# Decoder layer with a product-key expert FFN on one core: the second expert product over lists of experts in use, with rows fetched by index

## The chip, the core and the metric

The kernel runs on one core of a Trainium2 chip. The metric is the device time of one execution in microseconds (us). A run of the program is also profiled; the span in the profile goes from the first to the last instruction and is a little shorter than the time of the execution that it belongs to.

## What is computed

The reference is one decoder layer on 256 tokens of width 1024 (two attention-like mixers, a projection, a LayerNorm, then the expert FFN). The change is in the expert FFN. Each token has 8 heads; each head picks 16 of 16,384 experts by product keys, so there are 256 x 128 = 32,768 (token, expert, gate) choices:

```
s = einsum('thpk,pnk->thpn', q, sub_keys)              # two halves p, 128 keys n
top_s, top_i = top_k(s, 16)
cand_s = top_s[:, :, 0, :, None] + top_s[:, :, 1, None, :]     # 16 x 16 candidates
cand_i = top_i[:, :, 0, :, None] * 128 + top_i[:, :, 1, None, :]
best_s, best_pos = top_k(cand_s, 16)
experts = take_along_axis(cand_i, best_pos);  gates = softmax(best_s)
hid = gelu(einsum('chkd,cd->chk', u_tab[experts], x))
y   = einsum('chk,chkd->cd', gates * hid, v_tab[experts])
```

Then e = (p @ W_ple) * sigmoid(h @ W_pg + b_pg), and the output is LayerNorm(alpha * h + f + e), with f the y above.

## The kernel before

All weights are streamed. A unit of streaming is an *item* of 512 KB: `do_load` (L92) brings it from DRAM into a tile `raw` (4 buffers), `do_hi` (L103) makes its high part `hi` on ScalarE (ACT; line L110) and `do_lo` (L113) the low part `lo = raw - hi` on VectorE (DVE; line L123). A product of two float32 operands is three TensorE (PE) matmuls, hi*hi, hi*lo and lo*hi (`mm3`, L180), into PSUM. The program is a list of *steps*, one per item. The emission loop at the end writes, for each step, the loads, high parts (3 steps ahead) and low parts (2 steps ahead) by `advance`, then the step's matmuls, then what follows the step before. There is no scheduler: the order of the text is the order on each engine.

Work beside the stream comes in two ways. `stages` holds generators that go on by one `yield` per step. `queue` holds generators that yield an estimate of their DVE time; `run_queue(AUX_BUDGET)` lets each step take so much of it.

The steps in order: v, u, values, q/k, four projections, the output projection (`w_out`, 8 steps; its `wo_before` first finishes all `stages`), the per-layer gate (`w_pg`, 8 steps), the expert queries (`w_q`, 16 steps), the first expert product (128 steps) and the second (128 steps).

First expert product, `uexp_mm`: step i computes u_(i,j) . h_t for the 128 experts (i, j), all 256 tokens, with 24 matmuls of 256 columns; GELU (L802) puts two steps' result into the table H in SBUF. During `w_q` and the first half of these steps `topk_task` (two tasks, one for each 128 tokens) finds the experts and gates.

Gates, `g_task`: for 16 tokens at a time DVE builds one-hot matrices (A over j, B over i, times the gate in two float16 parts Bh and Bl: L815 to L822), PE multiplies them (L828, L829) to a dense gate matrix, and DVE multiplies that into H (L833). There are 32 such tasks, half of them beside the last 64 steps of the first product, half beside the first 64 steps of the second.

Second expert product: step i takes V rows of experts (i, 0..127) as one plain 512 KB load, `wsplit` makes high and low parts of H for two steps (L144 on ACT, L145 on DVE; tiles `wsp_*`), and `vexp_mm` (L885) does 12 matmuls of 512 columns: 2 token tiles x 2 column halves x 3. All 128 steps run, whether an expert is in use or not. The last 3 items are multiplied token tile by token tile, and LayerNorm 2 follows.

All loads and stores are issued by SyncE (SP, "SPq" in the profile); GpSimd (POOL) issues none.

## Time and profile before

| | |
|---|---|
| median of 3 runs | 1099.8 us (1099.3 to 1100.41) |
| span of the profiled execution | 1097.7 us |
| PE busy | 1085.3 us (99%), granted clock 0.997 of full |
| DVE busy | 819.3 us (75%) |
| ACT busy | 522.3 us (48%) |
| POOL busy | 4.4 us |
| moved by DMA | 205.3 MB, 187 GB/s |

The profile shows one execution. The profiled execution's own time is not given apart from its span; the median of the runs is 2.1 us above the span. Busy time counts instructions and not bytes; matmuls are pipelined, so the duration of one (282 ns) is longer than the distance between two starts.

### The profile page before, as it was taken

The page shows a single profiled execution, that of the slowest core. Times are in us where ns is not written, and L with a number is a line of the kernel's source. Part 1 is how long each engine was busy: PE and PEld are TensorE (multiplying, and loading weights), DVE is VectorE, ACT ScalarE, POOL GpSimd, SP SyncE. Part 2 cuts the span into 40 slices and gives each one's busy share as a digit, 9 for nine tenths or more (in the row PEclk, how much of TensorE's full clock was granted, in tenths as well). Part 3 has the DMA queues.
Part 4 walks back from the last instruction along what each step waited for, and adds up shares of the span by engine and source line. Part 5 has one row for each costly group of instructions (what it writes and reads, how often), then busy time and mean ns, then how long its engine had stood idle before and what let it go on. Part 6 is the DMA issues. An engine that isn't in the chain of part 4 may idle for free.

```text
span 1097.7 us, 19871 instructions
## 1 busy us (share of the span) xinstructions
PE 1085.3 (99%) x7985; PEld 989.4 (90%) x7985; DVE 819.3 (75%) x1429; ACT 522.3 (48%) x689; POOL 4.4 (0%) x7
## 2 busy tenths in 40 slices
PE   8999999999999999999999999999999999999996
PEld 6989999988999999999999999988888888888885
DVE  6875656577788989994878787689898975555556
ACT  6535655545445544454444434444444444444442
POOL 0000000000000000000000000000000000000000
PEclk9999999999999999999999999999999999999998
DMA  7856456774645556555555555554555555755551
GB/s 274 306 175 239 146 167 195 255 244 151 213 158 172 189 175 195 190 189 179 171 174 173 173 161 174 173 182 159 178 169 173 173 175 190 268 189 185 186 189 58
DMA packets 58576, 205.30 MB, mean 187 GB/s; under 512 B 6603, under 2 KB 8948, under 8 KB 58100
## 3 DMA queue, kind: packets, MB, share of 16 engines
q1 hardware_dynamic: 58484, 204.04, 56.5%
q8 instruction: 62, 1.02, 0.4%
q14 instruction: 30, 0.25, 0.1%
HBM read 201.91 MB, written 3.68 MB: 187 GB/s over the span
## 4 chain that ended last, share of the span: by engine, by line
PE 98%; DVE 1%; DMA 1%; SPq 0%; ACT 0%; issue 0%; DVEq 0%
PE acc L182 60%; PE y L885 32%; PE misc L828 1%; PE misc L829 1%; PE misc L694 1%; DMA raw<-in_w_v 1%; PE misc L388 0%; PE misc L488 0%; PE misc L466 0%; SPq L99 0%; DVE end L963 0%; PE misc L483 0%; DVE est L954 0%; DVE end L953 0%; PE misc L465 0%; PE misc L489 0%
## 5 line engine op out<-in xcount | busy, mean ns | idle before, releaser
L110 ACT CAST hi<-raw 128x1024 fp32r<-128x1024 f32 (+1 forms) x362 | 378.7, 1047 | 455.3 <-PE acc L182 219.5
L123 DVE TENSOR_TENSOR lo<-raw,hi 128x1024 fp32r<-128x1024 f32 (+1 forms) x362 | 440.2, 1218 | 151.6 <-PE acc L182 55.0
L182 PE MATMUL acc<-h_hi,hi 128*128 128x256 f32 x1152 | 324.9, 282 | 0.0
L182 PE MATMUL acc<-h_lo,hi 128*128 128x256 f32 x1152 | 322.2, 280 | 0.0
L182 PE MATMUL acc<-h_hi,lo 128*128 128x256 f32 x1152 | 321.9, 279 | 0.0
L182 PEld LDWEIGHTS acc<-h_hi,hi 128*128 128x128 f32 x1152 | 216.5, 188 | 0.0
L182 PEld LDWEIGHTS acc<-h_lo,hi 128*128 128x128 f32 x1152 | 216.4, 188 | 0.0
L182 PEld LDWEIGHTS acc<-h_hi,lo 128*128 128x128 f32 x1152 | 216.1, 188 | 0.0
L885 PE MATMUL y<-hi,wsp_hl 128*128 128x512 f32 x512 | 168.9, 398 | 0.0
L885 PE MATMUL y<-hi,wsp_hh 128*128 128x512 f32 x496 | 163.4, 398 | 0.0
L885 PEld LDWEIGHTS y<-hi,wsp_hl 128*128 128x128 f32 x512 | 96.4, 188 | 23.3
L885 PEld LDWEIGHTS y<-hi,wsp_hh 128*128 128x128 f32 x496 | 93.4, 188 | 22.5
L885 PE MATMUL y<-lo,wsp_hl 128*128 128x512 f32 x256 | 100.7, 393 | 0.0
L885 PE MATMUL y<-lo,wsp_hh 128*128 128x512 f32 x248 | 97.5, 393 | 0.0
L182 PE MATMUL acc<-xh,hi 128*128 128x256 f32 x320 | 92.2, 288 | 0.0
L182 PE MATMUL acc<-xh,lo 128*128 128x256 f32 x320 | 90.6, 283 | 0.0
L182 PE MATMUL acc<-xl,hi 128*128 128x256 f32 x320 | 90.6, 283 | 0.0
L182 PEld LDWEIGHTS acc<-xl,hi 128*128 128x128 f32 x320 | 61.5, 192 | 0.2
L182 PEld LDWEIGHTS acc<-xh,hi 128*128 128x128 f32 x320 | 61.4, 192 | 0.2
L182 PEld LDWEIGHTS acc<-xh,lo 128*128 128x128 f32 x320 | 61.4, 192 | 0.0
L815 DVE TENSOR_TENSOR A<-iota,dup_j 128x1024 f16<-128x1024 f16 x64 | 43.9, 686 | 20.1 <-PE misc L829 20.1
L885 PEld LDWEIGHTS y<-lo,wsp_hl 128*128 128x128 f32 x256 | 48.3, 189 | 10.6
(210 smaller groups left out, 1257.3 us busy)
## 6 DMA issues: line engine op xcount, KB each, us to landing
raw<-in_peer_uT SPq DMA_DIRECT2D x128, 512.0 KB, 3.8
raw<-in_peer_v SPq DMA_DIRECT2D x128, 512.0 KB, 4.2
raw<-in_w_qk SPq DMA_DIRECT2D x16, 512.0 KB, 4.3
raw<-in_w_q SPq DMA_DIRECT2D x16, 512.0 KB, 4.0
raw<-in_w_u SPq DMA_DIRECT2D x8, 512.0 KB, 6.1
raw<-in_w_vv SPq DMA_DIRECT2D x8, 512.0 KB, 4.6
raw<-in_w_pa SPq DMA_DIRECT2D x8, 512.0 KB, 3.7
raw<-in_w_ga SPq DMA_DIRECT2D x8, 512.0 KB, 4.2
```

What stands on the lines that cost most here:

```text
L110: nc.scalar.copy(parts[i][0][:, c], raws[i][:, c])
L123: nc.vector.tensor_sub(lo[:, c], r[:, c], hi[:, c].bitcast(F32))
L182: nc.tensor.matmul(ps, l, r, start=start and i == 0, stop=stop and i == 2)
L694: nc.tensor.matmul(sp[:, t, :], q[:, t * 128:(t + 1) * 128], keysT[:, j % 2, :], start=True, stop=True)
L815: nc.vector.tensor_tensor(v4(A), io(0, 128), bcs("j", 128), op=OP.is_equal)
L828: nc.tensor.matmul(ps[:, t, :], A[:, t, :], Bh[:, t, :], start=True, stop=False)
L829: nc.tensor.matmul(ps[:, t, :], A[:, t, :], Bl[:, t, :], start=False, stop=True)
L885: nc.tensor.matmul(cell["Y"][t][c], w[:, wp, j, t * 128:(t + 1) * 128], v[q][:, c, :], start=i == 0 and wp == 0 and q == 0, stop=i == NK - ...
```

## The change

1. A table HG in DRAM holds, for each expert and token tile of 128 tokens, 128 values of gelu(u.h) and 128 gates. `fill_task`, a stage from step 16 on, writes zeros to the gate half: 43 times two DMAs of up to 128 x 3 pieces of 512 bytes (192 KB), one pair every second step; what is left when `wo_before` finishes all stages is issued there.
2. GELU results go to HG by two DMAs per two steps (`uexp_post`, L970) instead of a tile in SBUF.
3. `topk_task` hands out results after 4 and after 8 heads. `scatter_gates` issues, on POOL, one indirect DMA with addition per (head, k): 128 gates of 4 bytes to 128 addresses. That is 4 batches of 64; the first DMA of a head waits until all 16 of the head before have landed.
4. `mask_task` makes one-hot matrices of the chosen experts on DVE (64 of 128x1024) and multiplies them on PE (256 matmuls of 128 columns): how often each token tile uses each expert. `list_task` turns that into three lists (used by tile 0 alone, by tile 1 alone, by both), numbers the members by triangular matmuls, and `slot_rows` (128 matmuls and 256 small DVE instructions) writes for each list position the expert's row number. Both go through `queue`, whose budget is now 1.45.
5. `w_pg` is split: 4 steps stay, 4 come after the first expert product.
6. The second expert product has 102 steps (*slots*): 50 for experts used by both tiles, 26 for each list of one tile, in the order both, tile 0, both, tile 1. A slot's 128 rows of V come by an indirect DMA on POOL (`do_load`, L114), its rows of HG by another (`hg_load`, L1010, 6 slots ahead). `wprep` multiplies gate and value on DVE (L1019) and splits the product (L164 on ACT, L165 on DVE). A slot of both has 12 matmuls, a slot of one tile 6.
7. From the first `w_pg` step on there are 11 raw buffers instead of 4 (`ring`). V rows are not asked for before the lists exist (`load_cap`).
8. If the list of both is longer than 50 slots, a branch (`overflow`, `tc.If`) works off up to 78 more slots one by one. Its condition is a count read into a register of every engine.
9. The dense gate matrix (`g_task`) and the tiles H are gone. The residual `res` stays in SBUF instead of going to DRAM and back.

The diff, cut to its core (lines with "..." stand for what is left out):

```diff
+NX = NK * NK
+ROWS = NX + 128
+ROW = 2 * T
+CAP_A, CAP_B = 26, 50
+SLOTS = 2 * CAP_A + CAP_B
+COLG = 8
+LISTG = 4
+FILL = 3
+HG_AHEAD = 6
+RING = 7
...
-AUX_BUDGET = 1.35
+FILL_AT = 16
+AUX_BUDGET = 1.45
...
-            r = stream.tile(items[i][1], F32, name="raw", tag="raw", bufs=RAW_BUFS)
-        for c in cuts(i):
-            nc.sync.dma_start(r[:, c], items[i][0][:, c])
+            pool, tag, bufs = ring[ring_pos[0] % len(ring)]
+            ring_pos[0] += 1
+            r = pool.tile(items[i][1], F32, name=tag, tag=tag, bufs=bufs)
+        if i in row_lists:
+            nc.gpsimd.indirect_dma_start(r.rearrange("p a b -> p (a b)"), None, items[i][0],
+                                         bass.IndirectOffsetOnAxis(ap=row_lists[i](), axis=0))
+        else:
+            for c in cuts(i):
+                nc.sync.dma_start(r[:, c], items[i][0][:, c])
...
-            while done["load"] <= last and sum(i not in x_items for i in range(done["lo"], done["load"])) < RAW_BUFS:
+            end = last if load_cap[0] is None else load_cap[0]
+            while done["load"] <= end and sum(i not in x_items for i in range(done["lo"], done["load"])) < len(ring):
...
+    HG = dram.tile([ROWS, 2, 2, 128], F32, name="HG")
+    def fill_task():
+        for r in (slice(0, 1), slice(NX + 1, ROWS)):
+            n = r.stop - r.start
+            nc.sync.dma_start(HG[r, :, 0, :], zero[:n, None, :].to_broadcast([n, 2, 128]))
+        rows = HG[:, :, :, :].rearrange("(p r) t w c -> p r t w c", p=128)
+        for r in range(0, ROWS // 128, FILL):
+            n = min(FILL, ROWS // 128 - r)
+            for t in range(2):
+                nc.sync.dma_start(rows[:, r:r + n, t, 1, :], zero[:, None, :].to_broadcast([128, n, 128]))
+            yield
+            yield
...
+        nc.sync.dma_start(kc, a["kc"])
+        nc.sync.dma_start(kcol, a["kcol"])
...
-        cell["H"] = {}
-        h0, cell["h0_es"] = open_pool("h0")
-        cell["h0"] = h0
-        cell["H"][0] = h0.tile([128, HALF, T], F32, name="H0", tag="H0")
+        more, cell["more_es"] = open_pool("more")
+        cell["more"] = more
+        ring.extend([(more, "raw2", RING)] * RING)
+        ring_pos[0] = len(ring) - RING
...
+    def scatter_gates(t, hf, gidx, gates):
+        for h in range(4 * hf, 4 * hf + 4):
+            before, scattered[t] = scattered[t], []
+            for k in range(TOPK):
+                c = TOPK * h + k
+                ins = nc.gpsimd.indirect_dma_start(
+                    gview[TOPK * t + k].rearrange("r t w (c o) -> (r t w c) o", o=1),
+                    bass.IndirectOffsetOnAxis(ap=gidx[:, c:c + 1], axis=0),
+                    gates[:, c:c + 1], None, compute_op=OP.add).ins
+                if k == 0:
+                    for p in before:
+                        tc.add_manual_dep(ins, p, SYNC, reason="another head may add to the same gate")
+                scattered[t].append(ins.name)
...
+            nc.vector.scalar_tensor_tensor(ex, ij[:, 0, :], float(NK), ij[:, 1, :], op0=OP.mult, op1=OP.add)
+            nc.vector.tensor_scalar(gidx[:, cc], ex, float(ROW), kcol[:, t:t + 1], op0=OP.mult, op1=OP.add)
+            scatter_gates(t, hf, gidx, gates.rearrange("p a b -> p (a b)"))
+            yield 0.2
...
+    def mask_task():
+        counts = bank((128, 2, 128))
+        cell["counts"] = counts
+        v4 = lambda x: x.rearrange("p t (i two) -> p t i two", two=2)
+        io = iota.rearrange("p (i two) -> p i two", two=2)[:, None].to_broadcast([128, COLG, 64, 2])
+        todo = None
+        for g in range(2 * 128 // COLG + 1):
+            new = None
+            if g < 2 * 128 // COLG:
+                t, c0 = divmod(g * COLG, 128)
+                new = [t, c0]
+                for p, n in ((1, "A"), (0, "B")):
+                    oh = tk.tile([128, COLG, 128], F16, name=n, tag=n, bufs=2)
+                    nc.vector.tensor_tensor(v4(oh), io, pairs[t][:, p, c0:c0 + COLG, None, :].to_broadcast(
+                        [128, COLG, 64, 2]), op=OP.is_equal)
+                    new.append(oh)
+                    yield 0.7
+            if todo:
+                t, c0, A, B = todo
+                for c in range(COLG):
+                    nc.tensor.matmul(counts[:, t, :], A[:, c, :], B[:, c, :], start=c0 + c == 0,
+                                     stop=c0 + c == 127)
...
+    def slot_rows(kdiv, kmod, n, rows, pair):
+        ps = bank()
+        todo = None
+        for i0 in range(0, NK + LISTG, LISTG):
+            new = None
+            if i0 < NK:
+                P, S = pair(i0)
+                for k in range(LISTG):
+                    i = i0 + k
+                    nc.vector.tensor_scalar(P[:, k, :], iof, kmod[:, i:i + 1], None, op0=OP.is_equal)
+                    nc.vector.tensor_scalar(S[:, k, :n], iof[:, :n], kdiv[:, i:i + 1], evals[:, i:i + 1],
+                                            op0=OP.is_equal, op1=OP.mult)
+                yield 1.0
+                new = (i0, P, S)
+            if todo:
+                j0, P, S = todo
+                for k in range(LISTG):
+                    nc.tensor.matmul(ps[:, :n], P[:, k, :], S[:, k, :n], start=j0 + k == 0, stop=j0 + k == NK - 1)
+            todo = new
+        nc.vector.tensor_copy(rows, ps[:, :n])
+
...
+        cell["vrow"] = cell["more"].tile([128, SLOTS], U32, name="vrow")
+        cell["grow"] = cell["more"].tile([128, SLOTS], U32, name="grow")
+        nc.vector.tensor_scalar(cell["vrow"], rows, -1.0, 0.0, op0=OP.add, op1=OP.max)
+        for t in range(2):
+            c = slice(CAP_A * t, CAP_A * (t + 1))
+            nc.vector.tensor_scalar(cell["grow"][:, c], rows[:, c], 2.0, float(t), op0=OP.mult, op1=OP.add)
+        nc.vector.tensor_copy(cell["grow"][:, 2 * CAP_A:], rows[:, 2 * CAP_A:])
+        load_cap[0] = None
...
-    def g_task(pair, hf):
...
-                nc.tensor.matmul(ps[:, t, :], A[:, t, :], Bh[:, t, :], start=True, stop=False)
-                nc.tensor.matmul(ps[:, t, :], A[:, t, :], Bl[:, t, :], start=False, stop=True)
...
-            hv = cell["H"][hf][:, :, t0:t0 + TOKG]
-            nc.vector.scalar_tensor_tensor(hv, ps.rearrange("p t i -> p i t"), 1.0 / GSC, hv,
-                                           op0=OP.mult, op1=OP.mult)
...
+        h = cell["more"].tile([128, 2, T], F32, name="hid", tag="hid", bufs=3)
+        nc.scalar.activation(h, ps, AF.Gelu)
+        for k in range(2):
+            r = (i - 1 + k) * NK + 1
+            nc.sync.dma_start(hview[r:r + NK, :, 0, :], h[:, k, :].rearrange("p (t c) -> p t c", t=2))
...
+    def v_open():
+        drain_queue()
+        cell["tk_es"].close()
+        vp, cell["vp_es"] = open_pool("vp")
+        cell["vp"] = vp
+        cell["end"] = vp.tile([128, 2, 2, D], F32, name="end")
+        row_bcast(cell["end"][:, 1, 0], a["ln2_g"])
+        row_bcast(cell["end"][:, 1, 1], a["ln2_b"])
+        for n in range(HG_AHEAD):
+            hg_load(n)
+
+    rhs_section(pg_items(1), lambda: cell["hh"], lambda: cell["hl"], 8, pg_post, ps=bank, cs0=1,
+                after={0: v_open, 2: lambda: wprep(0), 3: lambda: wprep(1)})
...
+    lists = [[(2, 2 * CAP_A + k) for k in range(CAP_B)], [(0, k) for k in range(CAP_A)],
+             [(1, CAP_A + k) for k in range(CAP_A)]]
+    while any(lists):
+        for k in (0, 1, 0, 2):
+            if lists[k]:
+                slots.append(lists[k].pop(0))
+    TOKS = ((0,), (1,), (0, 1))
...
+    def hg_load(n):
...
+        nc.gpsimd.indirect_dma_start(dst, None, src, bass.IndirectOffsetOnAxis(ap=cell["grow"][:, s:s + 1], axis=0))
+        hgs[n] = hg
...
+    def wprep(n):
+        m = len(TOKS[slots[n][0]])
+        hg = hgs.pop(n)
+        w = cell["vp"].tile([128, 2, 2, 128], F32R, name="wsp", tag="wsp", bufs=3)
+        hv = hg[:, :m, 0, :]
+        nc.vector.tensor_mul(hv, hv, hg[:, :m, 1, :])
+        split_to(w[:, 0, :m], w[:, 1, :m], hv)
+        wsp[n] = w
...
+        with tc.If(cell["reg"] > 0):
...
+        if n == SLOTS - EARLY:
+            overflow()
+        if n == 8:
+            cell["reg"] = nc.values_load(cell["extra"][0:1, 0:1], min_val=0, max_val=NX)
...
+        if n + HG_AHEAD < SLOTS:
+            hg_load(n + HG_AHEAD)
+        if n + 2 < SLOTS:
+            wprep(n + 2)
...
+    vit = []
+    for n, (kind, s) in enumerate(slots):
+        vit.append(add_item(a["peer_v"], [128, 2, 512]))
+        row_lists[vit[n]] = lambda s=s: cell["vrow"][:, s:s + 1]
+        step(vit[n], lambda n=n: vexp_mm(n), None, lambda n=n: vexp_before(n))
+    load_cap[0] = vit[0] - 1
```

The order in which instructions stand on the engines, at three places. First POOL, the whole program before (sgu is the masked spatial weights, end the last LayerNorm's tile):

```order
L354 ISA
L354 AFFINE_SELECT sgu<-sgu 128x1024
L976 TENSOR_TENSOR end<-end 128x512 x2
L1051 UNCONDITIONAL_BRANCH
L1051 ISA
```

And of the change, from the same place to the first slots of the second product:

```order
L394 AFFINE_SELECT sgu<-sgu 128x1024
L748 DMA HG<-gates_3309,gidx_3310 8454144x1 x128
L748 DMA HG<-gates_4761,gidx_4762 8454144x1 x128
L114 DMA raw_9134<-in_peer_v,vrow 128x1024
L114 DMA raw_9164<-in_peer_v,vrow 128x1024
L114 DMA raw_9199<-in_peer_v,vrow 128x1024
L114 DMA raw_9229<-in_peer_v,vrow 128x1024
L114 DMA raw_9264<-in_peer_v,vrow 128x1024
L114 DMA raw<-in_peer_v,vrow 128x1024 x4
L114 DMA raw_9424<-in_peer_v,vrow 128x1024
L1010 DMA hg<-HG,grow 128x512
L1010 DMA hg<-HG,grow 128x256
```

POOL now has all 256 scatters of gates, then ten gathers of V rows, then the gathers from HG, and after them V and HG in turn for each slot, 460 DMAs in all.

Second SP, around the start of the output projection (`w_out`), before:

```order
L535 DMA xn<-in_xn 128x2048
L99 DMA raw<-in_w_pb 128x1024
L99 DMA raw<-in_w_out 128x1024 x7
L216 DMA bc_l1g<-in_ln_g 128x1024
L216 DMA bc_l1b<-in_ln_b 128x1024
L216 DMA bc_pgb<-in_ple_b_gate 128x1024
L558 DMA iota<-in_iota 128x128
L559 DMA keysT<-in_keysT 128x256
L99 DMA raw<-in_w_out 128x1024
L99 DMA raw<-in_w_pg 128x1024 x8
```

and of the change:

```order
L118 DMA raw<-in_w_out 128x1024 x2
L279 DMA HG<-zero 128x3x128 x30
L236 DMA bc_l1g<-in_ln_g 128x1024
L236 DMA bc_l1b<-in_ln_b 128x1024
L236 DMA bc_pgb<-in_ple_b_gate 128x1024
L598 DMA iota<-in_iota 128x128
L599 DMA keysT<-in_keysT 128x256
L600 DMA kc<-in_kc 128x512
L601 DMA kcol<-in_kcol 128x2
L118 DMA raw<-in_w_out 128x1024
L118 DMA raw<-in_w_pg 128x1024 x4
```

Thirty zero fills (5.9 MB) stand ahead of the constants, of the eighth item of `w_out` and of `w_pg`.

Third DVE in the second product. Before, beside the gate tasks (lo is the low part of V, wsp_* the low part of H for two steps):

```order
L123 TENSOR_TENSOR lo<-raw,hi 128x1024 x2
L833 SCALAR_TENSOR_TENSOR H_2919<-misc,H_2919 128x64x8
L815 TENSOR_TENSOR A<-iota,dup_j 128x1024
L817 TENSOR_TENSOR B<-iota,dup_i 128x512
L820 TENSOR_TENSOR Bh<-B,dup_gh 128x512
```

and of the change, two slots (hg is the pair of gate and value, wsp the split product):

```order
L142 TENSOR_TENSOR lo<-raw,hi 128x1024
L1019 TENSOR_TENSOR hg<-hg 128x2x128
L165 TENSOR_TENSOR wsp<-hg,wsp 128x256
L142 TENSOR_TENSOR lo<-raw,hi 128x1024
L1019 TENSOR_TENSOR hg<-hg 128x128
L165 TENSOR_TENSOR wsp<-hg,wsp 128x128
```

The gate tasks are gone from there; every slot now has a multiplication, and behind it a subtraction that needs the high part which ACT makes of the product.

## Rows read from the trace of the kernel before

**Rows 1.** The page, part 1: busy us (share of the span), x instructions
```profile
PE 1085.3 (99%) x7985; PEld 989.4 (90%) x7985; DVE 819.3 (75%) x1429; ACT 522.3 (48%) x689; POOL 4.4 (0%) x7
```

**Rows 2.** Waits of PE: engine, tile, line <- releaser: us, times, longest
```profile
PE acc L308 <- DVE warm L305: 1.3, 1, 1.3
...
```

**Rows 3.** Chain that ended last: start us, us, engine, tile, line, xcount
```profile
399.70 96.12 PE acc L182 x816
...
531.01 8.56 PE acc L182 x72
540.53 11.39 PE acc L182 x96
...
713.37 14.00 PE y L885 x60
...
894.92 189.09 PE y L885 x810
```

**Rows 4.** PE timeline, end of `w_out` and keys' product: start us, us
```profile
251.84 0.39 PE L182 MATMUL acc<-pleh,ph 128*128 128x512 f32 x1
...
303.39 0.61 PE L694 MATMUL misc<-keysT,pq 128*128 128x128 f32 x4
303.75 0.36 PE L182 MATMUL acc<-h_hi,hi 128*128 128x256 f32 x1
303.96 0.28 PE L182 MATMUL acc<-h_lo,hi 128*128 128x256 f32 x1
```

**Rows 5.** DVE timeline in two stretches: start us, us, [idle before <-releaser]
```profile
61.09 0.43 DVE L145 TENSOR_TENSOR al<-at,ah 128x256 fp32r<-128x256 f32 x1 [0.47 <-ACT ah L144]
61.43 1.22 DVE L123 TENSOR_TENSOR lo<-raw,hi 128x1024 fp32r<-128x1024 f32 x1
62.57 0.42 DVE L394 TENSOR_TENSOR at<-misc,sgu 128x256 f32<-128x256 f32 x1
...
905.09 0.69 DVE L145 TENSOR_TENSOR wsp_hh<-H,wsp_hh 128x512 fp32r<-128x512 f32 x1 [0.83 <-ACT wsp_hh L144]
905.78 1.23 DVE L123 TENSOR_TENSOR lo<-raw,hi 128x1024 fp32r<-128x1024 f32 x1
```

**Rows 6.** Groups by line, shapes apart: xcount | busy us, mean ns | idle before
```profile
L144 ACT CAST ah<-at 128x256 fp32r<-128x256 f32 x8 | 3.3, 407 | 16.9 <-DVE at L396 16.9
L144 ACT CAST wsp_hl<-H 128x512 fp32r<-128x512 f32 x32 | 19.7, 615 | 0.0
L468 DVE SCALAR_TENSOR_TENSOR l<-misc,btab 128x128 f32<-128x128 f32 x8 | 2.3, 292 | 7.4 <-PE misc L466 4.2 <-DMA btab<-d 3.1
L478 DVE TENSOR_SCALAR l<-l,ast 128x128 f32<-128x128 f32 x8 | 2.3, 287 | 0.3
L479 DVE TENSOR_SCALAR l<-l,ast 128x256 f32<-128x256 f32 x8 | 2.8, 347 | 0.0
L976 POOL TENSOR_TENSOR end<-end 128x512 f32<-128x512 f32 x2 | 2.5, 1265 | 1046.9 <-ACT end L975 1046.9
```

**Rows 7.** Windows: stretch us, busy of PE, PEld, DVE, ACT, POOL, clock, DMA share, GB/s
```profile
80.00:84.00 4.00, 4.00 (x36) 4.00 (x35) 3.49 (x7) 0.58 (x2) 0.00 (x0) 1.00 0.98 345
200.00:240.00 40.00, 40.00 (x296) 38.31 (x296) 26.21 (x38) 19.10 (x25) 0.00 (x0) 1.00 0.73 241
400.00:420.00 20.00, 20.00 (x172) 20.00 (x171) 19.31 (x71) 9.98 (x14) 0.00 (x0) 1.00 0.56 178
```

**Rows 8.** SP's queue around the output projection: start us, us
```profile
225.78 6.10 SPq L99 DMA_DIRECT2D raw<-in_w_out  x3
231.94 0.42 SPq L216 DMA_DIRECT2D bc_l1g<-in_ln_g  x1
```

**Rows 9.** DMA issues: xcount, KB each, median us to landing
```profile
out_dram<-end SPq DMA_DIRECT2D x4, 256.0 KB, 2.0
```

**Rows 10.** SP's own time for one issue: ns min/median/max
```profile
L99 SPq DMA_DIRECT2D raw<-in_peer_v x128: 327/328/328, 696.7 to 1069.5; - x128
```

**Rows 11.** First instruction of DVE after the program's start
```profile
0.87 0.06 DVE L244 MEMSET eps<- 128x1 f32 x1 [0.87 <-PEq L1047]
```

More of the change, by code (lines that the diff above doesn't have):

```diff
@@ L86, in add_item @@
         return len(items) - 1
+    ring.extend([(stream, "raw", RAW_BUFS)] * RAW_BUFS)
     def cuts(i):
@@ L245, in block_kernel, with rhs_section @@
     bcol = lambda sec, fc: cols[:, sec * 8 + fc:sec * 8 + fc + 1]
-    def rhs_section(its, lh, ll, nk, post, before=None, early=0, after={}):
+    def rhs_section(its, lh, ll, nk, post, before=None, early=0, after={}, cs0=0, ps=None):
         state = {}
@@ L708, in topk_task @@
         bp = tk.tile([128, 8, TOPK], U32, name="bp")
+        gates = tk.tile([128, 8, TOPK], F32, name=f"gates{t}")
+        gidx = tk.tile([128, 128], U32, name=f"gidx{t}")
+        pairs[t] = tk.tile([128, 2, 128, 2], F16, name=f"pairs{t}")
         def top16(vals, idx, rows):
@@ L876, in vexp_mm @@
-    def vexp_mm(it, i, only=None):
-        v = parts[it]
-        w, j = wsp[i]
-        for t in range(2):
+        step(uit[i], lambda i=i: uexp_mm(uit[i], i), (lambda i=i: uexp_post(i)) if i % 2 else None)
+    def v_open():
[8 more added lines that the diff above has]
+            hg_load(n)
@@ new lines, in block_kernel @@
+    last = [max(n for n, s in enumerate(slots) if t in TOKS[s[0]]) for t in range(2)]
+    def hg_load(n):
+        kind, s = slots[n]
+        hg = cell["vp"].tile([128, 2, 2, 128], F32, name="hg", tag="hg", bufs=HG_AHEAD + 1)
+        if kind == 2:
+            dst, src = hg.rearrange("p t w c -> p (t w c)"), HG[:, :, :, :].rearrange("r t w c -> r (t w c)")
+        else:
+            dst, src = hg[:, 0].rearrange("p w c -> p (w c)"), HG[:, :, :, :].rearrange("r t w c -> (r t) (w c)")
+        nc.gpsimd.indirect_dma_start(dst, None, src, bass.IndirectOffsetOnAxis(ap=cell["grow"][:, s:s + 1], axis=0))
+        hgs[n] = hg
@@ L880, in vexp_mm @@
+    def wprep(n):
[6 more added lines that the diff above has]
+        wsp[n] = w
+    def vexp_mm(n, only=None):
+        v = parts[vit[n]]
+        w = wsp[n]
+        for j, t in enumerate(TOKS[slots[n][0]]):
             for wp in range(2):
@@ L884, in vexp_mm @@
                     for q in range(2 - wp):
-                        nc.tensor.matmul(cell["Y"][t][c], w[:, wp, j, t * 128:(t + 1) * 128], v[q][:, c, :],
-                                         start=i == 0 and wp == 0 and q == 0, stop=i == NK - 1 and wp == 1)
+                        nc.tensor.matmul(cell["Y"][t][c], w[:, wp, j, :], v[q][:, c, :],
+                                         start=(t, c) not in started, stop=n == last[t] and wp == 1)
+                        started.add((t, c))
@@ L947, in block_kernel @@
         for c in range(2):
-            for i in range(NK - EARLY, NK):
-                vexp_mm(vit[i], i, only=(t, c))
+            for n in range(SLOTS - EARLY, SLOTS):
+                vexp_mm(n, only=(t, c))
     def ln_sum(t, c):
```

273 lines of the change are left out of this document (142 added, 131 removed).

## The prediction

> **What bounds the kernel now.** I read the page first. The reader is to see that PE is busy for 1085.3 of 1097.7 us, and that no other engine comes near it [rows 1]. The waits of PE confirm it: the longest is 1.3 us, at the start [rows 2]. The chain that ended last says the same: it runs through PE's matmuls of the first product (96.12 us for 816, so 0.1178 us for one of 256 columns) and of the second (189.09 us for 810, so 0.2334 us for one of 512) [rows 3]. The clock is granted at 1.00 in every window that I read [rows 7], so a matmul left out is worth its spacing. I then looked at what stands close behind: DVE, 19.31 us of 20 in the first product beside the gate tasks, with PE full [rows 7]; and POOL, with 7 instructions in all [rows 1]. The change takes work from PE and gives POOL 460 DMAs; these two facts make the forecast and its risk.
>
> **What PE loses and gains.** The second product had 128 steps x 12 matmuls = 1536. It has 50 x 12 + 52 x 6 = 912. The 624 left out are worth 624 x 0.2334 = 145.6 us. The gate bursts go: the chain stops at 539.57 (531.01 + 8.56) for one and goes on at 540.53, 0.96 us each, 32 of them: 30.7 us [rows 3]. A few transposes of the top-k go too, 0.6 us by my count. What comes:
> - Counts: 256 float16 matmuls of 128 columns in 32 bursts of 8. A burst of 32 with 64 columns took 0.96 us, 0.03 each, so I take 0.06 for 128 columns, and 0.09 us per burst for leaving and entering the stream (next point): 32 x (8 x 0.06 + 0.09) = 18.2 us.
> - Row numbers of the slots: 32 bursts of 4 float32 matmuls. In the keys' product, four records (two such matmuls with 128 columns) ran from 303.39 to 303.75, 0.36 us, 0.18 each; the next stream matmul came 0.21 us before its follower instead of 0.12, so the change costs 0.09 [rows 4]. 32 x (4 x 0.18 + 0.09) = 26.0, and 2.7 for the few that number the members: 28.7 us.
>
> Sum on PE: -145.6 - 30.7 - 0.6 + 18.2 + 28.7 = -130.0. If PE stays the bound everywhere the span is 1097.7 - 130.0 = 967.7 us.
>
> **DVE in the second product.** A slot of both now passes: low part of V, multiplication, high part on ACT, subtraction. The low part of 1024 columns starts the next one after 1.14 us (61.43 to 62.57); a two-input instruction of 256 takes 0.43, of which 0.34 until the next starts; a hand-over is about 0.03 [rows 5]. ACT's cast of 256 takes 0.41, and from 0.615 for 512 I get 0.30 for 128; a two-input DVE instruction of 128 takes 0.29 [rows 6]. The subtraction stands right behind the multiplication on DVE, so DVE waits for ACT:
> - both: 1.14 + 0.43 + 0.03 + 0.41 + 0.03 + 0.34 (to 0.43) = 2.38 to 2.47;
> - one tile: 1.14 + 0.29 + 0.03 + 0.30 + 0.03 + 0.21 (to 0.29) = 2.00 to 2.08.
>
> A pair is 4.38 to 4.55; I take 4.5. PE needs 18 x 0.2334 = 4.20 for it. So DVE becomes the bound: 51 x 4.5 = 229.5, and six residual additions of about 0.69 (as wsp, [rows 5]) add 4.1: 233.6 us against 912 x 0.2334 = 212.8. DVE starts some 4 us ahead of PE, and behind its last part lie 18 matmuls, 4.2 us; they cancel. The term is +21, from 15 (4.38) to 27 (4.62), and 0 if ACT's cast hides behind other DVE work.
>
> **The fill.** Fills before `w_out` are hidden: about 11 MB from 70 to 231 us are 68 GB/s beside 241, 309 together [rows 7], under the 345 that the queue reached there. But 30 fills stand together where `wo_before` runs. Before, SP's third load of a burst went out near 231.5 and the constants followed at 231.94 [rows 8]; now 30 x 0.197 = 5.9 MB, 1.6 MB of broadcasts, 0.3 of constants and the eighth item of 0.52 stand in a row, 8.3 MB, 24 us at 345 GB/s. The item lands near 256. Its 24 matmuls ended at 251.84, where the gate's product begins [rows 4]; they began 24 x 0.2334 = 5.6 us earlier, at 246.2, and with some 2 us for the high and low parts the raw item was needed near 244. I add +12: 8 if the queue empties faster, 29 if pieces of 512 bytes go at half rate. SP's issue time (30 x 0.33, [rows 10]) is inside.
>
> The Trainium skill's page "DMA: Bandwidth & Descriptors" (section "Specifications") gives 512 bytes as the smallest transfer for line rate; no row here shows such a piece, and by it the 12 would stand.
>
> **Small terms.** With the queue's budget at 1.45 a step of DVE's work in the first half of the first product grows from 1.59 to 1.71 us in my count, 2.85 with the low part against 2.83 for 24 matmuls of 0.1178 [rows 3]: +2 (0 to 6). The overflow branch and its register load on each engine: the nearest row is DVE's 0.87 us behind the program's first branch [rows 11]; two such stops, +2 (0.9 to 5). The branch is not taken: counting the reference's own choices, 3316 experts are used by tile 0 alone, 3315 by tile 1 alone (room for 3328), 6069 by both (room for 6400).
>
> Hidden, at no cost: table writes, 16.8 MB in some 409 us, 41 GB/s beside 164, and behind loads that run 11 items ahead; V rows and HG rows, 66.4 MB in the second product, 192 us at 345 GB/s against 234. If that cover failed, every 10 GB/s less would cost 6 us.
>
> Sum: 967.7 + 21 + 12 + 2 + 2 = 1004.7 us of span. The median before lies 2.1 us over the span of its profile, so **1007 us**.
>
> **What POOL costs.** No row shows an indirect DMA. POOL executes 256 scatters and 204 gathers, one for each column of 128 indices. Let c be its time for one. Below: SP's 0.33 us per issue [rows 10]. Above: 2.0 us, a whole landing [rows 9]. The one POOL row of size is 1.265 us for 128x512 elements [rows 6]. I take the middle of the two bounds, 1.16.
>
> Let U0 be the first step of the first product, near 336 (V's start at 713.37 [rows 3] less 128 x 2.83 and 16 bursts). The four batches of 64 gates come at U0 + 20, 65, 111 and 156, and at c = 1.16 a batch takes 64 x 1.16 + 4 x 2.0 (a head waits for the one before to land) = 82: the last scatter ends at U0 + 20 + 4 x 82 = 348, before the lists are ready at about U0 + 374. V opens at U0 + 420 and would end at U0 + 633 by PE, 654 by DVE. After the lists 204 gathers remain, 187 of them inside V: 187 x 1.16 = 217 against 234, hidden. POOL without a pause ends at 20 + 32 (landings of 16 heads) + 8 (landing and last slot) + 460c = 60 + 460c. That is 654 at c = 1.29; in V alone the limit is 1.25. So the chosen value is hidden with a margin of a tenth only, and this is the largest risk.
>
> **Rivals.**
> - *DVE's chain hides* (the cast lies under the next low part): 1007 less 21, and with the fill at 8, about 982. For it: DVE was busy for 75% only [rows 1]; against: the order puts the subtraction right behind the multiplication. 0.15.
> - *POOL binds the second product*, c about 1.4: end 60 + 644 = 704, 71 behind PE's 633: 1007 - 21 + 71 = 1057. For it: each scatter is 128 separate pieces of 4 bytes; 1.265 is near the limit. 0.18.
> - *DVE holds POOL up.* `slot_rows` has 256 TENSOR_SCALARs of about 0.21 us start to start. They run at double rate: 128 columns more cost 60 ns (287 to 347), 0.47 ns a column, while a two-input one goes from 0.29 us for 128 to 1.23 for 1024, 1.05 ns a column [rows 5, 6]. If POOL stands still under them, 54 us: the limit falls from 1.29 to 1.17, and at c = 1.3 the end is 712, 1065 us. 0.06. Beside it stands the Trainium skill's page "SBUF — State Buffer", section "Who interferes with whom": in its two-port modes DVE takes the ports that GpSimd uses to write descriptors, and GpSimd waits. The double rate agrees with the first half; POOL issued no DMA here, so no run yet shows the second.
> - *Slower than before.* POOL's price alone decides: from 60 + 460c = 633 + 114, c = 1.49, the time passes 1099.8. At 1.6 it is 796, 163 behind PE: 1149; at the bound of 2.0, 980: 1333 us. For it: a landing of 2.0 us is of that size if POOL can't overlap issues; against: only the first scatter of a head has such a wait. 0.14.
> - *It doesn't do what it says:* the branch is taken, 78 rounds one behind another of some 11 us. The counts above speak against it. 0.02, slower.
>
> The Trainium skill's "DMA: Bandwidth & Descriptors", section "Latency and other measured facts", puts about 1 us of emission before the first byte of a GpSimd DMA. By it, as an estimate, POOL ends at U0 + 520 and the sum would stay; no row here can show it.
>
> **Numbers.** My forecast has 0.45, its own range 994 to 1037 by the bounds of its terms. Faster holds 0.45 + 0.15 + 0.18 + 0.06 = 0.84; slower 0.14 + 0.02, of which I give 0.01 to same, that is within 0.2%, about what a measurement of this kernel can tell from no change. Hence 0.84, 0.01, 0.15. The range goes from 968 (PE alone) to 1085 (c = 1.46), and leaves some 0.04 below and 0.16 above.
>
> **What would show it.** PE: 912 matmuls of y at 0.2334 spacing, if PE still sets the pace; the bursts of counts and rows near 0.6 and 0.8 us. DVE: in the second product some 0.4 us of idle time ahead of each wsp, put down to ACT, and PE's waits in it on DVE. SP: 30 fills in one run near 232, and one PE wait of about 12 us for the eighth `w_out` item. POOL: spacing of the scatters and gathers below 1.25 us; if PE or DVE wait in V for a gather instead, c is larger and one of the three POOL cases holds. The forecast is wrong most of all if POOL is still scattering when the lists are ready.

## The result, and the profile after

The changed kernel takes 1275.8 us (median of 4, 1275.06 to 1278.06) beside 1100.0 for the kernel before (median of 4): 1.160 times as long, interval 1.159 to 1.162. My 1007 was wrong by 269 us and on the wrong side; of the cases that I had named it is the slower one, POOL's price, at 0.14.

The first view is the page's part 1, as in [rows 1], and of its part 2 the busy tenths of PE and POOL and the granted clock in 40 slices of 32 us:

```profile
PE 985.8 (77%) x6867; PEld 895.6 (70%) x6867; DVE 767.0 (60%) x1597; ACT 493.4 (39%) x709; POOL 712.4 (56%) x467
...
PE   9999999759999999999999990000008877878875
...
POOL 0000000000058788777888787777777777877782
PEclk9999999979999999999999995555558999898998
```

PE's work fell as it should, from 1085.3 to 985.8 us busy (954.4, or 130.9 less, in a run below in which PE hardly waits), but its share fell to 77%. POOL rose from 4.4 to 712.4 us. The row of PE has a hole in slices 25 to 30, while POOL stands at 7 or 8 from slice 13 to the last but one. The granted clock drops to 0.5, the lower of its two levels (1.2 GHz), in that hole, where PE has hardly any work, and comes back when it has.

The waits of PE (engine, tile, line <- releaser: us, times, longest), where [rows 2] had 1.3 us at most:

```profile
PE y L1032 <- ACT wsp L164: 248.9, 38, 194.9
PE acc L202 <- ACT hi L129: 20.3, 2, 19.5
```

One wait of 194.9 us stands ahead of the second product, and 54 us in 37 pieces within it. ACT's `wsp` is only the last to come; by the groups of ACT and DVE it waits for DVE's product, and DVE for the rows of HG:

```profile
L164 ACT CAST wsp<-hg 128x256 fp32r<-128x256 f32 (+1 forms) x102 | 35.8, 351 | 176.4 <-DVE hg L1019 164.7
L1019 DVE TENSOR_TENSOR hg<-hg 128x256 f32<-128x256 f32 (+1 forms) x102 | 36.3, 356 | 75.1 <-DMA hg<-HG,grow 72.8
```

The other row of PE's waits is the eighth item of `w_out`: 19.5 us, where I had put 12.

POOL's timeline (start us, us, [idle before <- releaser]), at the first scatters, the last ones, the first gathers and within the second product:

```profile
363.03 2.44 POOL L748 DMA_INDIRECT HG<-gates,gidx  x1 [320.74 <-DVE gidx L835]
365.77 2.23 POOL L748 DMA_INDIRECT HG<-gates,gidx  x1 [0.30 <-issue]
...
404.56 1.89 POOL L748 DMA_INDIRECT HG<-gates,gidx  x1 [3.25 <-DMA HG<-gates,gidx]
...
938.87 1.54 POOL L748 DMA_INDIRECT HG<-gates,gidx  x1 [0.30 <-issue]
940.72 1.00 POOL L114 DMA_INDIRECT raw<-in_peer_v,vrow  x1 [0.30 <-issue]
...
953.50 0.96 POOL L1010 DMA_INDIRECT hg<-HG,grow  x1 [0.30 <-issue]
...
1014.73 0.97 POOL L114 DMA_INDIRECT raw<-in_peer_v,vrow  x1 [0.30 <-issue]
1016.01 1.78 POOL L1010 DMA_INDIRECT hg<-HG,grow  x1 [0.30 <-issue]
```

The last scatter ends at 940.4, where the lists had been ready since about 712 (the last matmul of their row numbers starts at 711.5). POOL's groups by line (xcount | busy us, mean ns | idle before) give the price that no row before could give:

```profile
L748 POOL DMA_INDIRECT HG<-gates,gidx x256 | 463.1, 1809 | 435.0 <-DVE gidx L835 320.7 <-issue 73.3 <-DMA HG<-gates,gidx 40.6
L1010 POOL DMA_INDIRECT hg<-HG,grow x102 | 131.3, 1288 | 31.1 <-issue 28.3 <-DMA raw<-in_peer_v,vrow 1.2 <-DVE wsp L165 1.2
L114 POOL DMA_INDIRECT raw<-in_peer_v,vrow x102 | 113.2, 1110 | 32.4 <-issue 15.5 <-ACT wsp L164 5.9 <-DVE lo L142 3.4
```

A scatter is busy for 1.81 us, and 0.30 us pass before the next, so 2.1 us; with 40.6 us of waits between heads the 256 take 577.7 us (363.03 to 940.72), 2.26 each. A gather takes 1.11 or 1.29 and 0.30: the 204 of them fill 940.72 to 1248.5, 1.51 each. My c was 1.16.

Last, the windows of the second product (stretch, busy of PE, PEld, DVE, ACT, POOL, clock, DMA share, GB/s):

```profile
790.00:970.00 180.00, 9.48 (x31) 7.26 (x32) 10.26 (x17) 8.84 (x13) 141.01 (x99) 0.52 0.31 47
985.00:1090.00 105.00, 84.11 (x315) 62.02 (x315) 63.75 (x106) 45.70 (x70) 83.80 (x70) 0.93 0.75 240
```

In 985 to 1090 POOL's 83.8 us in 70 instructions and 70 gaps of 0.30 make 104.8 of 105 us. No other engine is full: POOL sets the pace.

### The profile page after: what moved, and what is told of

The parts are those of the page before. It is cut to its first block, busy times and chain, and to the rows that moved or that the text cites. A ratio compares the mean times of both kernels' runs of the same rounds, so it can differ in the third digit from the quotient of the medians.

```text
span 1273.9 us, 18586 instructions
## 1 busy us (share of the span) xinstructions
PE 985.8 (77%) x6867; PEld 895.6 (70%) x6867; DVE 767.0 (60%) x1597; ACT 493.4 (39%) x709; POOL 712.4 (56%) x467
## 5 line engine op out<-in xcount | busy, mean ns | idle before, releaser
L748 POOL DMA_INDIRECT HG<-gates,gidx x256 | 463.1, 1809 | 435.0 <-DVE gidx L835 320.7
L142 DVE TENSOR_TENSOR lo<-raw,hi 128x1024 fp32r<-128x1024 f32 (+1 forms) x336 | 406.9, 1212 | 276.4 <-ACT hi L129 217.3
L1032 PE MATMUL y<-hi,wsp 128*128 128x512 f32 x608 | 219.1, 431 | 250.4 <-ACT wsp L164 248.9
L1032 PEld LDWEIGHTS y<-hi,wsp 128*128 128x128 f32 x608 | 123.7, 204 | 301.6 <-ACT wsp L164 273.0
L1010 POOL DMA_INDIRECT hg<-HG,grow x102 | 131.3, 1288 | 31.1 <-issue 28.3
L114 POOL DMA_INDIRECT raw<-in_peer_v,vrow x102 | 113.2, 1110 | 32.4 <-issue 15.5
L1032 PE MATMUL y<-lo,wsp 128*128 128x512 f32 x304 | 127.7, 420 | 0.0
L164 ACT CAST wsp<-hg 128x256 fp32r<-128x256 f32 (+1 forms) x102 | 35.8, 351 | 176.4 <-DVE hg L1019 164.7
L1019 DVE TENSOR_TENSOR hg<-hg 128x256 f32<-128x256 f32 (+1 forms) x102 | 36.3, 356 | 75.1 <-DMA hg<-HG,grow 72.8
L1032 PEld LDWEIGHTS y<-lo,wsp 128*128 128x128 f32 x304 | 62.1, 204 | 13.0
L165 DVE TENSOR_TENSOR wsp<-hg,wsp 128x256 fp32r<-128x256 f32 (+1 forms) x102 | 36.6, 359 | 47.8 <-ACT wsp L164 46.4
```

Of the source, the lines that this page charges most:

```text
L114: nc.gpsimd.indirect_dma_start(r.rearrange("p a b -> p (a b)"), None, items[i][0], bass.IndirectOffsetOnAxis(ap=row_lists[i](), axis=0))
L142: nc.vector.tensor_sub(lo[:, c], r[:, c], hi[:, c].bitcast(F32))
L164: nc.scalar.copy(hi, src)
L165: nc.vector.tensor_sub(lo, src, hi.bitcast(F32))
L748: ins = nc.gpsimd.indirect_dma_start(gview[TOPK * t + k].rearrange("r t w (c o) -> (r t w c) o", o=1), bass.IndirectOffsetOnAxis(ap=gidx[: ...
L1010: nc.gpsimd.indirect_dma_start(dst, None, src, bass.IndirectOffsetOnAxis(ap=cell["grow"][:, s:s + 1], axis=0))
```

## The experiments

**Whose time is it?** Three kernels take POOL's work away in parts.

`e1_no_scatter`:

```diff
-            scatter_gates(t, hf, gidx, gates.rearrange("p a b -> p (a b)"))
```

> The 256 scatters of gates are left out (so every gate is zero). Theory P, POOL's own price per indirect DMA: the second product can start as soon as its lists are there, near 765 instead of 960 us, and then runs at POOL's pace of two gathers per slot, 2.9 us a slot as now: about 765 + 295 + 15 = 1075 us. Rival D, the dependent chain of DVE and ACT sets the pace in the second product as I had predicted (4.5 us a pair): about 765 + 234 + 15 = 1015 us. Rival Q, the queue of 4-byte and 512-byte pieces slows every transfer, the V rows too: the time falls below 1015, towards PE's own 1000.

`e2_plain_rows`:

```diff
-            nc.gpsimd.indirect_dma_start(r..., None, items[i][0], ...)
+            nc.sync.dma_start(r..., items[i][0][k:k + 128])
...
-        nc.gpsimd.indirect_dma_start(dst, None, src, ...)
+        nc.sync.dma_start(dst, src[128 * s:128 * s + 128])
```

> All 256 scatters stay; the 204 gathers become plain loads on SP of the same number of rows and bytes from fixed places, so the product is taken of other rows. Theory P: the second product still starts near 943 to 960, and then runs at the DVE chain's 4.5 us a pair, 234 us instead of 298: about 1212 us. Rival Q (transfers, not POOL, set the pace of the second product): 298 us as before, 1276 us.

`e3_neither` has both edits.

> Neither scatters nor gathers on POOL (both edits above). It is my forecast without POOL's part: 1007 plus the 8 us that the fill took beyond my 12, so 1015 us, if the DVE chain paces the second product at 4.5 us a pair; 995 us if ACT's cast hides and PE paces it.

Measured: 1084.9 us without scatters, 1198.3 without gathers, 1017.5 with neither (before: 1100.4 on the same chip). Theory P said 1075, 1212 and 1015; D would have had 1015 in the first and Q 1276 in the second. Both fall. The first came out 10 us over theory P: its second product started at 767.3 and took 300 us, where I had 765 and 295, and some 2 us more lie behind it. Without gathers the second product also starts 10 us sooner (950.2), as no row of V or HG has to wait for its turn on POOL behind the last scatter, so 1198 and not 1212. Counted from 1017.5, the gathers cost 67 us, the scatters 181, and both together 258. A window and DVE's timeline with neither show why the second product then takes 233 us:

```profile
850.00:900.00 50.00, 50.00 (x203) 37.28 (x203) 39.80 (x68) 29.71 (x45) 0.00 (x0) 1.00 0.96 329
```

```profile
850.35 1.22 DVE L142 TENSOR_TENSOR lo<-raw,hi 128x1024 fp32r<-128x1024 f32 x1
851.49 0.28 DVE L1018 TENSOR_TENSOR hg<-hg 128x128 f32<-128x128 f32 x1
852.18 0.29 DVE L165 TENSOR_TENSOR wsp<-hg,wsp 128x128 fp32r<-128x128 f32 x1 [0.41 <-ACT wsp L164]
852.39 1.22 DVE L142 TENSOR_TENSOR lo<-raw,hi 128x1024 fp32r<-128x1024 f32 x1
853.52 0.42 DVE L1018 TENSOR_TENSOR hg<-hg 128x256 f32<-128x256 f32 x1
854.46 0.43 DVE L165 TENSOR_TENSOR wsp<-hg,wsp 128x256 fp32r<-128x256 f32 x1 [0.52 <-ACT wsp L164]
854.80 1.22 DVE L142 TENSOR_TENSOR lo<-raw,hi 128x1024 fp32r<-128x1024 f32 x1
```

The window has PE as busy all the time, but with 203 matmuls in 50 us, one in 0.246 us where 0.233 is its own spacing: it is DVE that holds it back, as `e8_pipe` below confirms. From one low part to the next but one (850.35 to 854.80) a pair of slots takes 4.45 us; I had 4.38 to 4.55 and took 4.5. The idle time ahead of each `wsp` is 0.41 and 0.52 us, put down to ACT, as forecast.

**One gather or two?** `e11_one_gather` has no scatters, keeps the gather of V rows and makes the load from HG plain.

```diff
-            scatter_gates(t, hf, gidx, gates.rearrange("p a b -> p (a b)"))
...
-        nc.gpsimd.indirect_dma_start(dst, None, src, ...)
+        nc.sync.dma_start(dst, src[128 * s:128 * s + 128])
```

> No scatters; V rows by gather on POOL, the rows of the table by plain loads on SP. Theory P: one gather a slot, 0.95 to 1.5 us and 0.3 between two, hides under the 2.23 us that DVE needs: the time is that of the run with neither, 1017 within 4. Rival R, the gathered rows themselves arrive late, one gather being as bad as two: 1040 or more.

Measured: 1020.9 us. One gather a slot is hidden, with rows that arrive in time; two are not. R falls. POOL's group:

```profile
L114 POOL DMA_INDIRECT raw<-in_peer_v,vrow x102 | 96.4, 945 | 837.6 <-DMA raw<-in_w_pg 690.8 <-ACT wsp L164 76.1 <-DVE hg L1018 45.1
```

These gathers are short, 0.945 us on average, although beside 87 of the 102 DVE subtracts a low part. POOL's and DVE's timelines show what is different here:

```profile
850.14 0.94 POOL L114 DMA_INDIRECT raw<-in_peer_v,vrow  x1 [1.09 <-DVE hg L1018]
...
850.57 1.22 DVE L142 TENSOR_TENSOR lo<-raw,hi 128x1024 fp32r<-128x1024 f32 x1
```

Each waits for a buffer, by ACT's `wsp` or DVE's product, and so, in the second product, it begins just before such a subtraction and not while one is running (of the short one of `wsp` at most 0.14 us are left). Why that matters is shown with the DVE probe below.

**What is in a scatter?** `e5_forms` changes the last heads of tile 1, which POOL scatters while DVE is idle.

```diff
+            few, plain = 64 if t and h >= 6 else 128, t and h in (5, 7)
...
-                    bass.IndirectOffsetOnAxis(ap=gidx[:, c:c + 1], axis=0),
-                    gates[:, c:c + 1], None, compute_op=OP.add).ins
+                    bass.IndirectOffsetOnAxis(ap=gidx[:few, c:c + 1], axis=0),
+                    gates[:few, c:c + 1], None, **({} if plain else {"compute_op": OP.add})).ins
```

> Of tile 1, heads 5 and 7 are scattered without addition and heads 6 and 7 with 64 indices instead of 128 (so some gates are overwritten and half of two heads is left out); these heads run where DVE is idle, in which a scatter of 128 with addition took 1.54 us and a gather of 128 rows 0.95. If the addition is the difference, heads 5 and 7 take 0.95; if a piece of 4 bytes is, they stay at 1.54. If POOL pays by the index, heads 6 and 7 take about half, 0.8 or less; if it pays by the instruction, they don't change. The time falls by at most 64 x 0.7 = 45 us.

Measured: 1255.8 us. POOL's timeline, one scatter of each of the heads 4 to 7:

```profile
831.51 1.56 POOL L749 DMA_INDIRECT HG<-gates,gidx  x1 [0.30 <-issue]
...
862.35 0.96 POOL L749 DMA_INDIRECT HG<-gates,gidx  x1 [0.30 <-issue]
...
888.02 1.42 POOL L749 DMA_INDIRECT HG<-gates,gidx  x1 [0.30 <-issue]
...
913.33 0.91 POOL L749 DMA_INDIRECT HG<-gates,gidx  x1 [0.30 <-issue]
```

With addition 128 indices take 1.56 us and 64 take 1.42; without it 0.96 and 0.91. The addition costs 0.5 to 0.6 us per instruction, an index almost nothing (64 more make 0.05 us without addition and 0.14 with it): POOL pays by the instruction. A plain scatter costs what a gather does (0.95), though its pieces have 4 bytes and a gather's up to 4 KB, so it isn't the size of a piece either. Against 1.55 the three heads save 16 x (0.59 + 0.13 + 0.64) = 22 us, and the time fell by 20.

**Does DVE hold POOL up?** `e4_dve_probe` adds idle work beside the scatters.

```diff
+        for _ in range(24):
+            nc.vector.tensor_add(za, za, zb)
+        for _ in range(48):
+            nc.vector.tensor_add(za[:, :512], za[:, :512], pb)
+        for _ in range(48):
+            nc.vector.tensor_scalar(za, zb, 1.0, None, op0=OP.mult)
+        for _ in range(24):
+            nc.vector.tensor_reduce(junk, zb, axis=AX.X, op=OP.add)
```

> Four blocks of DVE instructions that compute nothing of use are added where DVE is idle beside the last scatters, 750 to 870 us: 24 TENSOR_TENSOR of 128x1024 with both inputs in SBUF, 48 of 128x512 with one input in PSUM, 48 TENSOR_SCALAR of 128x1024, 24 TENSOR_REDUCE. Theory P alone: each scatter takes 1.54 us (1.85 start to start) beside all four, and the time stays at 1276. Rival L, DVE holds POOL up: the scatters get longer beside one or two of the blocks, to 2 us or more; if only TENSOR_SCALAR does it, double-rate instructions are the cause, if only the first block does, two inputs from SBUF are. The time then rises by what the scatters lose, 5 to 30 us.

Measured: 1292.4 us. DVE's timeline gives the four blocks (`misc` is in PSUM), POOL's one scatter within each:

```profile
760.06 30.18 DVE L991 TENSOR_TENSOR end<-end 128x1024 f32<-128x1024 f32 x24
790.28 34.60 DVE L993 TENSOR_TENSOR end<-end,misc 128x512 f32<-128x512 f32 x48
824.92 34.91 DVE L995 TENSOR_SCALAR end<-end 128x1024 f32<-128x1024 f32 x48
859.75 30.06 DVE L997 TENSOR_REDUCE junk<-end 128x1 f32<-128x1024 f32 x24
```

```profile
775.59 2.21 POOL L748 DMA_INDIRECT HG<-gates,gidx  x1 [0.30 <-issue]
...
805.60 1.55 POOL L748 DMA_INDIRECT HG<-gates,gidx  x1 [0.30 <-issue]
...
836.92 1.88 POOL L748 DMA_INDIRECT HG<-gates,gidx  x1 [0.30 <-issue]
...
870.09 1.55 POOL L748 DMA_INDIRECT HG<-gates,gidx  x1 [0.30 <-issue]
```

Beside two inputs from SBUF a scatter takes 2.21 us, beside TENSOR_SCALAR 1.88, beside one input from PSUM and beside TENSOR_REDUCE 1.55, as with DVE idle. Within a block all scatters but those at its edges agree within 0.03. Rival L holds, for both kinds; P alone falls. The scatters' sum rose by 10 us (463.1 to 473.2 busy) and the time by 17; of the other 7, 2.3 lie ahead of the first scatter (365.32 beside 363.03) and 3.4 are idle time of POOL between scatters.

How DVE does it, single rows of the changed kernel show (DVE's and POOL's timelines):

```profile
748.31 1.22 DVE L142 TENSOR_TENSOR lo<-raw,hi 128x1024 fp32r<-128x1024 f32 x1 [1.58 <-PE acc L202]
748.46 2.49 POOL L748 DMA_INDIRECT HG<-gates,gidx  x1 [0.30 <-issue]
...
753.35 1.55 POOL L748 DMA_INDIRECT HG<-gates,gidx  x1 [2.40 <-DMA HG<-gates,gidx]
753.91 1.22 DVE L142 TENSOR_TENSOR lo<-raw,hi 128x1024 fp32r<-128x1024 f32 x1 [1.58 <-PE acc L202]
```

The first scatter begins while a subtraction is running and ends 1.42 us after that one does; in the second a subtraction begins, and it takes the 1.55 us of a quiet one. So it goes through the whole trace. 109 of the 256 scatters begin while a TENSOR_TENSOR with both inputs in SBUF is running, and take 2.14 us on average; the other 147 take 1.57, though such an instruction begins within 38 of them. Of the 204 gathers 138 begin so, with 1.31 us on average, and the other 66 take 0.96. What is lost is nearly always the rest of the one instruction that runs when the DMA begins, so it is no fixed sum. The probe's 2.21 us are 0.79 of rest and 1.42 of POOL's own, as scatters and additions fell into step there; a scatter at 761.18, which began 0.08 us before an addition ended, takes 1.54. Beside the TENSOR_SCALARs 0.34 us are rest, and 0.12 are lost later in each scatter.

`e6_lo_on_act` asks the same in the second product: no scatters, and no low part on DVE.

```diff
+            if i in row_lists:
+                nc.scalar.copy(lo[:, c], r[:, c])
+            else:
+                nc.vector.tensor_sub(lo[:, c], r[:, c], hi[:, c].bitcast(F32))
```

> Without scatters (as in the run before this one without them, 1084.9 us), and the low part of V made by a copy on ACT, so its values are wrong, and DVE has only the two small instructions of a slot. Theory L, DVE's instructions with two inputs from SBUF lengthen the gathers: they fall from a mean of 1.2 towards 0.95 us, a slot from 2.94 to about 2.6, the time to about 1050 us. Theory P alone (POOL's own price varies by itself, or with the load of the queue): the gathers stay at 1.2 us and the time at 1085.

Measured: 1039.1 us, 46 less than with DVE's low part. POOL's groups there, and in the run without scatters that it is to be compared with:

```profile
L1012 POOL DMA_INDIRECT hg<-HG,grow x102 | 98.3, 964 | 37.2 <-issue 13.4 <-DVE hg L1021 10.4 <-DMA end<-in_ln_g 6.4
L114 POOL DMA_INDIRECT raw<-in_peer_v,vrow x102 | 96.5, 946 | 733.0 <-DMA raw<-in_w_pg 688.4 <-issue 17.1 <-DVE lo L145 16.6
```

```profile
L1009 POOL DMA_INDIRECT hg<-HG,grow x102 | 127.1, 1246 | 36.4 <-issue 29.0 <-DMA end<-in_ln_g 5.6 <-DMA raw<-in_peer_v,vrow 1.2
L114 POOL DMA_INDIRECT raw<-in_peer_v,vrow x102 | 113.0, 1108 | 736.1 <-DMA raw<-in_w_pg 688.7 <-DVE lo L142 16.0 <-issue 15.8
```

The gathers fall from 1.25 and 1.11 us to 0.96 and 0.95. That is 0.44 us a slot, 45 us in 102 slots, of the 46 that the time fell by. So DVE's subtraction of 1024 columns, with both inputs in SBUF, was what lengthened them; it stands in every slot.

**The fill.** `e7_late_fill` spreads the fills that were left.

```diff
-            yield
-            yield
+            yield
+            if slow:
+                yield
...
         while stages:
             run_stages()
+        slow.clear()
...
         run_stages()
+        for g in fills:
+            next(g, None)
...
-            stages.append(fill_task())
+            fills.append(fill_task())
```

> The fills that were left are no longer issued in one run ahead of the output projection, but one pair a step, into the expert queries. Theory F, those 30 in a row held the eighth item of the output projection: PE's wait of 19.5 us goes, all that follows moves forward, POOL's chain too, and the time falls by 17 to 20 us, to 1257. Rival: POOL's scatters do not start earlier, because the top-k and not the fill sets their start by DVE's own speed, or later loads wait for the spread fills instead: less than 8 us.

Measured: 1253.3 us, 22.5 less. PE's wait for the eighth item is gone, and POOL's first scatter comes at 341.43 instead of 363.03, so the whole chain moves. In the changed kernel the run of 30 looks so in SP's timeline, and so in the windows:

```profile
233.61 20.70 SPq L279 DMA_DIRECT2D HG<-zero  x30
254.40 0.59 SPq L236 DMA_DIRECT2D bc_l1g<-in_ln_g  x1
...
258.54 0.43 SPq L601 DMA_DIRECT2D kcol<-in_kcol  x1
259.08 0.87 SPq L118 DMA_DIRECT2D raw<-in_w_out  x1
```

```profile
232.00:262.00 30.00, 16.07 (x71) 12.96 (x69) 9.71 (x13) 4.31 (x5) 0.00 (x0) 0.82 1.00 284
```

30 fills hold SP for 20.70 us, 5.9 MB or 285 GB/s with the queue full, where 345 was reached before [rows 7]. The time fell by 3 us more than PE's wait. Some 2 of them are the clock's: while PE waited, the granted clock fell to 0.50 (windows of 258 to 268), its lower level, and it was 0.55 in 268 to 272, when PE worked again, and 1.00 from 272 on; with the late fill it is 1.00 in all of this stretch.

**DVE's chain.** `e8_pipe` has no POOL DMAs, and multiplies a slot ahead; `e9_pipe_change` is the same edit on the full change; `e10_pe_floor` adds the late fill to `e8_pipe`.

```diff
         nc.vector.tensor_mul(hv, hv, hg[:, :m, 1, :])
-        split_to(w[:, 0, :m], w[:, 1, :m], hv)
+        nc.scalar.copy(w[:, 0, :m], hv)
...
         if n + 2 < SLOTS:
-            wprep(n + 2)
+            wprep_low(n + 2)
+        if n + 3 < SLOTS:
+            wprep(n + 3)
```

> Without scatters and gathers (as in the run with neither, 1017.5 us), and with the multiplication and ACT's cast of a slot one slot ahead of its subtraction, so that DVE no longer waits for ACT. If that wait was what made a pair 4.45 us, PE sets the pace again with 18 x 0.2334 = 4.20: 51 x 0.25 = 13 us less, and 4 of the tail, about 1002 us. Rival, transfers: the queue was busy to 0.96 there and moved 324 GB/s; if that is its limit the time stays at 1017, or falls by less than 5.

> The full change, with the multiplication and ACT's cast one slot ahead of the subtraction, the edit that gave 19.6 us (1017.5 to 997.8) where POOL had no part. Theory P, POOL sets the pace of the second product: nothing, 1276 within 4. Rival C, the chain DVE-ACT-DVE is part of the loop that holds the gathers' buffers: 10 to 20 us less.

> No scatters, no gathers, the multiplication a slot ahead and the fills spread: all that I had put above PE's own sum is taken away but branch and top-k. If the sum on PE, -130.0 us, was right, the time is 967.7 + 2 + 2 + 2.1 = 974, and by the two runs that had one of the edits each it is 997.8 - 22 = 976. Rival: transfers, at 345 GB/s in the second product already, take over, or the term of the row numbers was too small: 985 or more.

Measured: 997.8, 1273.0 and 977.2 us. The window of `e8_pipe` and the waits of PE in `e10_pe_floor`:

```profile
850.00:900.00 50.00, 50.00 (x215) 40.22 (x214) 40.74 (x73) 31.94 (x48) 0.00 (x0) 1.00 0.97 342
```

```profile
PE misc L524 <- issue: 1.6, 1, 1.6
```

The wait for ACT was worth 19.6 us (13 for the pairs and 4 for the tail were expected), and PE sets the pace again: 215 matmuls in 50 us, 0.2326 each. Transfers don't hold it, though they stand at 342 GB/s: the rival falls. On the full change the same edit moves the time by 3 us, which single runs can hardly tell from none: P holds, C falls. Without POOL, fills and the chain, 977.2 us are left, and no wait of PE over 1.6.

## Why the prediction was wrong

**What PE loses and gains** was right. The sum said 967.7 of span with PE full, 973.8 with branch, top-k and what lies around the span; `e10_pe_floor` has 977.2. PE's busy time is 954.4 there, 130.9 less than before. So -130.0 is right to some 4 us. The changed kernel has 912 matmuls of y (608 and 304), so the overflow branch was not taken, and that rival falls.

**DVE in the second product** was right where POOL leaves it alone: 4.45 us a pair measured, 4.5 used; +21 in the sum, 19.6 by `e8_pipe`.

**The fill** was right in place and cause, and mis-sized inside its bounds of 8 to 29: +12 forecast, 19.5 in the wait, 22.5 when it was undone. The step "at 345 GB/s" failed: these fills ran at 285, which makes 3.6 us. The run also began 1.7 us later than assumed (233.61 beside 231.94); the rest stays open. The Trainium skill's page "DMA: Bandwidth & Descriptors", section "Specifications", gives 512 bytes as the smallest transfer for line rate. The fills, in pieces of just that size, stayed below the 345 GB/s that the loads reached; whether it is the size of the pieces or that they are written to DRAM was not tried.

**Without POOL** the forecast stands then: 1007 plus 8 of the fill is 1015, and `e3_neither` took 1017.5.

**What POOL costs** is the step that failed: "I take the middle of the two bounds, 1.16." Five things are in it.
- A quiet gather takes 0.95 us, well inside the bounds; a quiet scatter with addition 1.55. One c for both was wrong, and I had counted the addition as nothing.
- The 0.30 us between two instructions stood nowhere in the sum: I had taken SP's 0.33 [rows 10] for a whole issue, where on POOL such a gap comes on top. So c is 1.25 quiet for a gather, above my 1.16 and at the limit of 1.25 that I had worked out for the second product, and 1.85 for a scatter.
- DVE adds to it: 463.1 - 256 x 1.547 = 67 us on the scatters, and 244.5 - 204 x 0.951 = 50 us on the gathers. Both lie on POOL's chain. I had priced only the TENSOR_SCALARs of `slot_rows`, as a rival.
- Waits between heads are 40.6 us, 32 forecast: mis-sized only.
- The two costs come one behind the other, since the gathers from HG need the last scatter. My formula had this. With the measured c of (577.7 - 40.6 + 308) / 460 = 1.84 it gives 60 + 846 = 906, 273 behind PE's 633, and 1007 - 21 + 273 = 1259; with 8 for the fill and 9 for the waits it comes to 1276, beside 1275.8; so close a fit is partly luck, since terms of a few us are left out. The mechanism was named, and the price decides: by the formula c lies beyond both limits, 1.29 and 1.49.

**The rival on DVE** was true in kind, with the wrong instructions and the wrong price. It had POOL stand still under the 256 small TENSOR_SCALARs of `slot_rows`, for 54 us. The rests of running instructions with two inputs from SBUF, added up over the trace, make 63 of the 67 us on the scatters and 49 of the 50 on the gathers, so those TENSOR_SCALARs cost less than 5. Of the instructions that hold POOL the low part, which stands in every step, is the commonest. The Trainium skill's page "SBUF — State Buffer", section "Who interferes with whom", says that a DVE instruction with two SBUF inputs contends with a GpSimd instruction that reads SBUF, and, as an inference, that TENSOR_TENSOR leaves the making of descriptors alone. The traces agree with both: a DMA waits for the TENSOR_TENSOR that runs when it begins (2.49 us at 748.46) and not for one that begins later (1.55 us at 753.35). That it is the reading of its indices that waits would fit, but no run shows it.

The Trainium skill's figure of about 1 us of emission, which I quoted from its page "DMA: Bandwidth & Descriptors", section "Latency and other measured facts", is near the quiet gather's 0.95 us. It is not the distance of two such DMAs in a row, 1.25 us when quiet, nor that of two scatters, 1.85; by it, as an estimate, the time would have stayed at 1007.

**Can the change be saved?** Not by the late fill and a DVE that is never in the way. With both, POOL's chain starts at 341.4, has 256 x 1.85 = 474 us of scatters, 41 of waits, 204 x 1.25 = 255 of gathers, and 25 behind the last gather: 1136 us of span, over the 1097.7 of before. This is an estimate from the rows above, not run. To get below it one needs an earlier start of the scatters, fewer DMAs, or scatters without addition. In the form used here, with one index per partition, 32,768 gates are 256 of them; and an addition that is left out needs gates whose addresses never meet, which the choices of several heads don't give. None of these was tried.
